# First chunk's down-projection by seven half-size products, its weight sums made in the mixer, its last norms after the second up phase

## The chip, the cores and the metric

The kernel runs on one core of one Trainium2 chip. The metric is the device time of one execution in microseconds (us). Engine names are those of the profile: PE is TensorE's matmuls, PEld its weight loads, DVE is VectorE, ACT is ScalarE, POOL is GpSimd, SP is SyncE, which issues most DMAs. Each engine runs its own queue of instructions in a fixed order and waits on semaphores.

## The reference, cut to what matters

One layer of a streaming encoder over 2048 positions with 1024 features, all in float32: a mixer (a linear recurrence and a gated spatial mixer), then a feed-forward part with a width-3 causal convolution. Each sub-layer is wrapped in two norms and a modulation computed from a vector `c`.

```python
h = rmsnorm(x, g_mix_pre[l]) * (1.0 + sc_m) + sh_m
z = h @ w_in[l]
...
y = y @ w_out[l]
x = x + gt_m * rmsnorm(y, g_mix_post[l])

h = rmsnorm(x, g_ffn_pre[l]) * (1.0 + sc_f) + sh_f
up = causal_depthwise_conv(h @ w_up[l], ffn_conv_w[l], ffn_conv_b[l])
g_ff, v_ff = jnp.split(up, 2, axis=-1)
y = (jax.nn.gelu(g_ff) * v_ff) @ w_down[l]
x = x + gt_f * rmsnorm(y, g_ffn_post[l])
```

The change touches the last three lines: the down-projection (3072 to 1024 features), the norm `g_ffn_post` behind it and the modulation `gt_f`.

## The kernel before, in words

Features lie on partitions, positions on the free axis. Every float32 matmul operand is split into a high and a low half (ACT casts the high half, DVE subtracts to get the low half, line 143), and a product is three matmuls: high by high, high by low, low by high.

The program has these stages. The mixer works in four chunks of 512 positions (about 0 to 680 us). The feed-forward part works in two chunks of 1024 positions, `C` = 0 and 1, each with an up phase (24 steps `f`; a step makes 128 gate and 128 value features, convolves them, applies gelu and multiplies) and a down-projection.

- The up phase multiplies 2 x 2 blocks by seven half-size products instead of eight (`up_pair`), except the first two steps of chunk 0 (`up_plain`). A step's result `gg` is stored to `gd` by SP (`gated`).
- Chunk 0's down-projection is plain (`down(0, t)`): for each half `t` of 512 positions, 24 steps of 8 output blocks, 3 matmuls each.
- Chunk 1's down-projection (`down_fast(1)`) uses seven products of half size. The block indices are even and odd feature blocks by output and position halves. Its products are called by their operands: "11" by "11", "s1" by "t1", "s2" by "t2", "s4" by "22", "s3" by "t3", "12" by "21", "22" by "t4". Each has 6 steps `q` of 24 matmuls (144 in all). They accumulate in two sets of four PSUM banks, `A` and `B`.
- The `s` operands are sums of gate products. `g_sums` makes them for chunk 1 on DVE in its up phase and stores them to `gsd`. The `t` operands are sums of weights. `w_sums` makes them on POOL and stores them to `wsd`: eight of the twelve pairs from the raw weights that the plain stage loads anyway (`W_SUMS`), four in the second up phase (`w_sums_apart`).
- `final` is the last norm: a reciprocal (line 206), eight scalings of 128x512 (line 1164), four adds of the residual (line 1169) and four stores. Chunk 0's first norm runs in the second plain half; its second one runs in the second up phase, from step 3 on, with its data read back from `od`.
- `ada_task(5, 1)` computes the modulation `gt_f`: eight passes of 128x1024 on DVE (line 280) with waits between them.

Work in the background is written as generators in a list; `tick()` advances each by one step, and `drain()` runs what is left to its end at that place. A scheduler then orders each engine's queue; `tc.high_priority(offset=...)` moves operands ahead. Buffers are pools of 4 KB per partition: 36 for general use (`t4`), 8 for split weights (`wp`), 4 for raw weights (`rw`), 3 for loads (`lp`). An instruction that reuses a buffer waits for its last reader.

Of the kernel before, what the change touches and what calls it, by code (L numbers as in the profile page):

```python
# [40 lines left out]
def block_kernel(ctx: ExitStack, tc: tile.TileContext, xt, cols, rows, wada, wada_r, win_k, win_s, win_v, wgate, wsp, wout, wup, wdown, out):  # L41
# [586 lines left out]


# [439 lines left out]
    W_SUMS = (7, 9, 11), (4, 5, 6, 8, 10)  # L1069
    done = []  # L1070
    od = dram.tile([P, ND, 512], F32, name="od")

    def down(C, t):


        n = f"{C}{t}"
        sl = slice(512 * t, 512 * t + 512)
        pts = {}
        G, W = {}, {}
        by_dram = t == 1  # L1080
        last_f = 2
        raws = {}

        def operands(f):
            if f % 2 == 0:
                with tc.high_priority(offset=150):
                    raw = rw.tile([P, 2, 512], F32, tag="wraw", name=f"gr{n}_{f}")
                    sync.dma_start(out=raw, in_=gd[C, :, f:f + 2, sl])
                    hl = [wp.tile([P, 2, 512], F32R, tag="w", name=f"g{q}{n}_{f}") for q in "hl"]
                    split(hl[0], hl[1], raw, "act")  # L1090
                for b in range(2):
                    G[f + b] = hl[0][:, b], hl[1][:, b]

            def mkraw(name):
                raws[f] = rw.tile([P, 8, P], F32, tag="wraw", name=name)
                return raws[f]

            W[f] = weight(wdown[f], [P, 8, P], f"wd{n}_{f}", ahead=150, mkraw=mkraw)
            if f % 2 and f // 2 in W_SUMS[t]:
                with tc.high_priority(offset=150):  # L1100
                    w_sums(f // 2, raws[f - 1], raws[f])

        def mm(f, d):
            if d not in pts:
                pts[d] = bank(f"dn{n}_{d}")
            wh, wl = W[f]
            mm3(pts[d], (wh[:, d], wl[:, d]), G[f], f == 0, f == NF - 1)

        O, acc = [], []

        def evict(d):
            if d % 2 == 0:
                O.append(t4(f"fo{n}_{d}"))
            acc.append(e_tile(f"fs{n}_{d}"))
            act.activation(out=acc[-1], in_=pts[d], func=AF.Square)
            o = O[-1][:, d % 2]
            act.copy(out=o, in_=pts[d])
            if d:
                vec.tensor_tensor(out=acc[0], in0=acc[0], in1=acc[-1], op=ALU.add)
            if by_dram and d % 2:  # L1120
                sync.dma_start(out=od[:, d - 1:d + 1], in_=O[-1])

        for f in range(2):
            operands(f)
            for d in range(7):
                mm(f, d)
            tick()
        while done:
            drain(done.pop(0))
# [289 lines left out]
```

## Time and profile before

| what | value |
|---|---|
| median of 3 runs | 2149.26 us (2148.96 to 2150.14) |
| profiled execution, its own time | 2147.84 us |
| its span | 2146.1 us |
| mixer, to the first up step | about 680 us |
| first up phase | about 680 to 1150 us |
| plain down-projection, both halves | 1150 to 1424 us |
| second up phase | 1424 to 1882 us |
| seven-product down-projection | 1890 to 2121 us |
| end of the last norm | 2146 us |

The span is the profiler's time from the first to the last instruction of that one execution; the median is of separate runs. Busy time of PE counts overlapping matmuls by their modelled ends, so PE's pace is read from the starts of neighbouring matmuls.

### The profile page before, as it was taken

The page shows a single profiled execution, that of the slowest core. Times are in us where ns is not written, and L with a number is a line of the kernel's source. Part 1 is how long each engine was busy: PE and PEld are TensorE (multiplying, and loading weights), DVE is VectorE, ACT ScalarE, POOL GpSimd, SP SyncE. Part 2 cuts the span into 40 slices and gives each one's busy share as a digit, 9 for nine tenths or more (in the row PEclk, how much of TensorE's full clock was granted, in tenths as well). Part 3 has the DMA queues.
Part 4 walks back from the last instruction along what each step waited for, and adds up shares of the span by engine and source line. Part 5 has one row for each costly group of instructions (what it writes and reads, how often), then busy time and mean ns, then how long its engine had stood idle before and what let it go on. Part 6 is the DMA issues. An engine that isn't in the chain of part 4 may idle for free.

```text
span 2146.1 us, 24188 instructions
## 1 busy us (share of the span) xinstructions
PE 2029.0 (95%) x8888; PEld 1667.2 (78%) x8888; DVE 1486.8 (69%) x1631; ACT 943.4 (44%) x1214; POOL 526.3 (25%) x322
## 2 busy tenths in 40 slices
PE   5897979999998999999999999999999999989995
PEld 3686868878877888787788887788888888868884
DVE  7787698697575688988987637745665555564556
ACT  3463643633644455554555434443333333353442
POOL 4355244343212234435330031430011110000000
PEclk8899989999999999999999999999999999999997
DMA  8587578677586679889875756657898887576645
GB/s 326 177 308 279 185 261 288 247 252 280 199 295 224 214 264 325 303 293 349 295 294 190 247 196 220 231 182 241 301 335 297 301 282 242 201 253 208 197 157 147
DMA packets 176359, 541.01 MB, mean 252 GB/s; under 512 B 16496, under 2 KB 16624, under 8 KB 176240
## 3 DMA queue, kind: packets, MB, share of 16 engines
q1 hardware_dynamic: 164176, 496.47, 66.5%
q0 software_dynamic: 10912, 38.80, 4.8%
q10 hardware_dynamic: 1152, 4.19, 0.5%
q8 instruction: 70, 1.15, 0.2%
q14 instruction: 49, 0.40, 0.1%
HBM read 355.90 MB, written 184.55 MB: 252 GB/s over the span
## 4 chain that ended last, share of the span: by engine, by line
PE 75%; DVE 11%; DMA 5%; issue 4%; ACT 4%; POOL 1%; SPq 0%; DVEq 0%; ACTq 0%; POOLq 0%
PE upa L980 7%; PE upa L982 7%; PE upa L981 7%; PE dA L1233 5%; PE dB L1233 5%; PE dn L179 4%; PE dn L181 4%; PE dn L180 4%; PE upc L980 3%; PE upc L981 3%; PE upc L982 3%; PE upb L981 2%; PE upb L982 2%; PE upb L980 2%; PE lg L179 1%
## 5 line engine op out<-in xcount | busy, mean ns | idle before, releaser
L929 DVE SCALAR_TENSOR_TENSOR a<-Rg,prm,a 128x1023 f32<-128x1023 f32 x92 | 128.9, 1401 | 97.8 <-ACT a L927 97.8
L929 DVE SCALAR_TENSOR_TENSOR a<-Rv,prm,a 128x1023 f32<-128x1023 f32 x92 | 133.0, 1445 | 23.3 <-ACT a L927 22.5
L179 PE MATMUL dn<-gh,wd_h 128*128 128x512 f32 x384 | 147.7, 390 | 1.2 <-ACT fr_r L205 0.8
L180 PE MATMUL dn<-gl,wd_h 128*128 128x512 f32 x384 | 147.3, 389 | 0.0
L181 PE MATMUL dn<-gh,wd_l 128*128 128x512 f32 x384 | 131.5, 390 | 2.3 <-DVE wd_l L143 2.3
L927 ACT ACTIVATE a<-Rv,prm 128x1024 f32<-128x1024 f32 x46 | 57.2, 1244 | 132.4 <-DVE Rv L1048 132.2
L143 DVE TENSOR_TENSOR wd_l<-wd_r,wd_h 128x1024 fp32r<-128x1024 f32 x48 | 59.6, 1244 | 75.8 <-ACT wd_h L138 69.2
L138 ACT CAST wd_h<-wd_r 128x1024 fp32r<-128x1024 f32 x48 | 50.5, 1056 | 129.8 <-PE dn L180 119.1
L1166 POOL DMA_DIRECT2D out_dram<-do x2 | 2.5, 1240 | 409.8 <-DVE do L1164 409.7
L960 POOL TENSOR_TENSOR wug<-wuv,wug 128x512 f32<-128x512 f32 x24 | 41.9, 1747 | 243.6 <-DVE w L143 243.6
L143 DVE TENSOR_TENSOR wt<-wug,wt 128x512 fp32r<-128x512 f32 x72 | 72.5, 1007 | 32.7 <-ACT wt L138 32.6
L985 ACT ACTIVATE a<-a 128x1024 f32<-128x1024 f32 x48 | 50.9, 1061 | 87.4 <-DVE a L929 46.9
L138 ACT CAST wt<-wug 128x512 fp32r<-128x512 f32 x72 | 44.9, 623 | 96.1 <-POOL wug L960 38.8
L181 PEld LDWEIGHTS dn<-gh,wd_l 128*128 128x128 f32 x384 | 71.8, 188 | 18.6 <-DVE wd_l L143 3.8
L179 PEld LDWEIGHTS dn<-gh,wd_h 128*128 128x128 f32 x384 | 72.1, 188 | 17.5 <-ACT wd_h L138 1.3
L180 PEld LDWEIGHTS dn<-gl,wd_h 128*128 128x128 f32 x384 | 72.1, 188 | 14.8
L1175 POOL TENSOR_TENSOR wsr<-wsr 128x512 f32<-128x512 f32 x4 | 5.2, 1296 | 251.5 <-DMA wsr<-in_wdown_dram 251.5
L222 POOL TENSOR_TENSOR rp_s<-rp_s,rp_s 128x1024 f32<-128x1024 f32 x12 | 31.4, 2618 | 116.2 <-ACT rp_s L218 116.0
L1175 POOL TENSOR_TENSOR wd_r<-wd_r 128x512 f32<-128x512 f32 x8 | 11.2, 1396 | 195.8 <-DVE wd_l L143 195.8
L927 ACT ACTIVATE a<-Rg,prm 128x1024 f32<-128x1024 f32 x46 | 57.1, 1242 | 1.3
L1048 DVE TENSOR_TENSOR Rv<-upa,m 128x512 f32<-128x512 f32 x46 | 31.5, 684 | 36.3 <-PE upa L982 36.3
L280 DVE SCALAR_TENSOR_TENSOR ada_m<-wada,cact,ada_m 128x1024 f32<-128x1024 f32 x28 | 47.8, 1706 | 11.9 <-DMA wada<-in_wada_r_dram 11.9
(648 smaller groups left out, 6695.8 us busy)
## 6 DMA issues: line engine op xcount, KB each, us to landing
wkd<-wt SPq DMA_DIRECT2D x88, 512.0 KB, 3.6
wkd<-w SPq DMA_DIRECT2D x66, 512.0 KB, 4.1
w<-wkd SPq DMA_DIRECT2D x66, 512.0 KB, 4.4
wd_r<-in_wdown_dram SPq DMA_DIRECT2D x48, 512.0 KB, 4.4
wrt<-wkd SPq DMA_DIRECT2D x44, 512.0 KB, 4.3
wt<-wkd SPq DMA_DIRECT2D x44, 512.0 KB, 4.6
wada<-in_wada_r_dram SPq DMA_DIRECT2D x32, 512.0 KB, 4.9
win_h<-kept_s SPq DMA_DIRECT2D x30, 512.0 KB, 6.0
```

The costliest lines, as they stand in the source:

```text
L138: act.copy(out=hi, in_=src)
L143: (leng or vec).tensor_tensor(out=lo, in0=src, in1=hi.bitcast(F32), op=ALU.subtract)
L179: pe.matmul(out=out, lhsT=wh, rhs=mh, start=first, stop=False)
L180: pe.matmul(out=out, lhsT=wh, rhs=ml, start=False, stop=False)
L181: pe.matmul(out=out, lhsT=wl, rhs=mh, start=False, stop=last)
L927: act.activation(out=a, in_=R, func=AF.Identity, scale=w[2], bias=col("ffn_conv_b", blk))
L929: vec.scalar_tensor_tensor(out=a[:, s:], in0=R[:, :FT - s], scalar=w[t], in1=a[:, s:], op0=ALU.mult, op1=ALU.add)
L980: pe.matmul(out=pt, lhsT=wh, rhs=mh, start=first and not more and k == 0, stop=False, skip_group_check=more)
L981: pe.matmul(out=pt, lhsT=wh, rhs=ml, start=False, stop=False, skip_group_check=more)
L982: pe.matmul(out=pt, lhsT=wl, rhs=mh, start=False, stop=last and k == 3, skip_group_check=more)
L985: act.activation(out=g, in_=g, func=AF.Gelu_apprx_tanh)
L1233: pe.matmul(out=pt, lhsT=x[:, a, d], rhs=y[:, a], start=first and z == 0, stop=stop and z == 2, skip_group_check=True)
```

## The change

1. `down`, `W_SUMS` and `w_sums_apart` go. Chunk 0 also uses `down_fast`.
2. `w_sums` becomes a background task of the mixer, started at its chunk 2, with its own loads of the weights into the raw-weight buffers `rw`.
3. `g_sums` also runs in chunk 0's up phase, and `gg` of chunk 0 moves into the load buffers `lp`.
4. In `down_fast(0)` the activations' raw tiles are in `t4` and their halves in the weight buffers `wp`. Results go to `od`, the sums of squares into one tile `fsum`. `h2_next` makes the second chunk's input sums in that stage.
5. `first_finals` (the modulation, then both last norms of chunk 0, their data read back from `od`) starts at step 3 of the second up phase. What of it is not reached by then comes out in a `drain()` ahead of `down_fast(1)`.
6. In the last product of chunk 1 the work of `then` starts one step earlier, and its tiles are taken when they are needed.

```diff
@@ mixer
+    def w_sums():
+        for p in range(NF // 2):
+            e, o = [rw.tile([P, 8, P], F32, tag="wraw", name=f"ws{p}_{i}") for i in range(2)]
+            sync.dma_start(out=e, in_=wdown[2 * p])
+            sync.dma_start(out=o, in_=wdown[2 * p + 1])
+            yield
+            pool.tensor_tensor(out=e[:, :4], in0=e[:, 4:], in1=e[:, :4], op=ALU.subtract)
...
+            pool.dma_start(out=wsd[p, 0], in_=e)
+            pool.dma_start(out=wsd[p, 1], in_=o)
+            yield
...
         if c == 2:
             m4, = start(ada_task(4, 1))
+            wst = start(w_sums())
@@ gated
-        o = lp.tile([P, 2, 512], F32, tag="ld", name=f"gg{C}_{f}") if C else g.rearrange("p (a c) -> p a c", a=2)
+        o = lp.tile([P, 2, 512], F32, tag="ld", name=f"gg{C}_{f}")
...
-        if C:
-            GG[f] = o
-            if f % 2:
-                start(g_sums(f // 2))
+        GG[f] = o
+        if f % 2:
+            start(g_sums(C, f // 2))
@@ down_fast, operands
-                raw = t4(f"dgr{n}") if first else lp.tile([P, 2, 512], F32, tag="ld", name=f"dgr{n}")
+                raw = t4(f"dgr{n}") if first or C == 0 else lp.tile([P, 2, 512], F32, tag="ld", name=f"dgr{n}")
                 sync.dma_start(out=raw, in_=a_src(op, q))
-                g = h4(f"dgh{n}"), h4(f"dgl{n}")
+                if C == 0:
+                    g = [wp.tile([P, 2, 512], F32R, tag="w", name=f"dg{x}{n}") for x in "hl"]
+                else:
+                    g = h4(f"dgh{n}"), h4(f"dgl{n}")
@@ down_fast, product
-                if q == 2 and then:
+                if q == (1 if held else 2) and then:
                     then()
@@ down_fast, end for chunk 0
+        if C == 0:
+            run("22", "t4", A, False, 0, lambda: combine(B, "m1", 0, 0))
+            combine(A, None, 1, 0)
+            return
@@ new
+    def first_finals():
+        yield from ada_task(5, 1)
+        vec.tensor_tensor(out=gf, in0=modc[:, 40:48], in1=colr("g_ffn_post", 0, 8), op=ALU.mult)
+        for t in range(2):
+            hl = rms_split(fsum[0][:, t], f"fr0{t}")
+            yield
+            yield from final(0, t, [None] * 4, hl)
...
+    def h2_next():
+        for i in range(2):
+            yield from wait(4)
+            g = h2_sums(1, i, from_x2(1, i), True)
+            for _ in g:
+                yield from wait(2)
@@ main
-    for t in range(2):
-        start(h2_sums(1, t, from_x2(1, t), True), *(() if t else (ada_task(5, 1),)))
-        down(0, t)
-        drain()
...
-    up_phase(1, 0, lambda f: start(done.pop(0)) if f == 3 else start(w_sums_apart()) if f == 8 else None)
+    start(h2_next())
+    down_fast(0)
+    drain()
+    up_phase(1, 0, lambda f: start(first_finals()) if f == 3 else None)
+    drain()
     down_fast(1)
     drain()
```

Three places show how the queues move. The first is DVE where the second up phase ends and the second chunk's first product begins. `a..` are convolution results, `dgl` and `dw.._l` the low halves of activations and weights (in the changed kernel with the chunk's number in front, so `dgl11_0` becomes `dgl111_0`), `gg` the step's product, `fr00` and `fr01` the first chunk's norm factors, `fo` its data and `fx` its residual. DVE before:

```order
L929 SCALAR_TENSOR_TENSOR a1_23_13622<-Rg1_23_13561,prm_81,a1_23_13622 128x1022
L934 SCALAR_TENSOR_TENSOR a1_23_13622<-ftails_4095,prm_81,a1_23_13622 128x2
L143 TENSOR_TENSOR dgl11_0_13657<-dgr11_0_13654,dgh11_0_13656 128x1024
L988 TENSOR_TENSOR gg1_23_13629<-a1_23_13622,a1_47_13603 128x1024
L143 TENSOR_TENSOR dw11_0_l_13663<-dw11_0_r_13660,dw11_0_h_13662 128x1024
L143 TENSOR_TENSOR dgl11_1_13699<-dgr11_1_13696,dgh11_1_13698 128x1024
L143 TENSOR_TENSOR dgl11_2_13735<-dgr11_2_13732,dgh11_2_13734 128x1024
```

DVE now, from the first reciprocal on:

```order
L206 RECIPROCAL fr00_r_13633<-fr00_r_13633 128x512
...
L1104 SCALAR_TENSOR_TENSOR fo00_0_13636<-fo00_0_13636,gf_109,fr00_r_13633 128x512 x2
...
L1104 SCALAR_TENSOR_TENSOR fo00_3_13660<-fo00_3_13660,gf_109,fr00_r_13633 128x512 x2
L1005 TENSOR_TENSOR gg1_23_13610<-a1_23_13603,a1_47_13584 128x1024
L206 RECIPROCAL fr01_r_13674<-fr01_r_13674 128x512
L143 TENSOR_TENSOR dgl111_0_13726<-dgr111_0_13723,dgh111_0_13725 128x1024
L1109 TENSOR_TENSOR fo00_0_13636<-fo00_0_13636,fx00_0_13638 128x1024
...
L1104 SCALAR_TENSOR_TENSOR fo01_0_13677<-fo01_0_13677,gf_109,fr01_r_13674 128x512 x2
...
L1104 SCALAR_TENSOR_TENSOR fo01_3_13701<-fo01_3_13701,gf_109,fr01_r_13674 128x512 x2
L143 TENSOR_TENSOR dw111_0_l_13732<-dw111_0_r_13729,dw111_0_h_13731 128x1024
...
L1109 TENSOR_TENSOR fo01_3_13701<-fo01_3_13701,fx01_3_13703 128x1024
L143 TENSOR_TENSOR dgl111_2_13798<-dgr111_2_13795,dgh111_2_13797 128x1024
```

Both norms now stand between the convolution and the low halves of the first product, and the low half of step 2's activations stands behind the last residual add.

The second place is SP's queue at the same seam; `dgr` and `dw.._r` are the raw loads, `out` the results. SP before:

```order
L1223 DMA dgr11_0_13654<-gd_99 128x2x512
L148 DMA dw11_0_r_13660<-in_wdown_dram 128x2x512
L1223 DMA dgr11_1_13696<-gd_99 128x2x512
L1223 DMA dgr11_2_13732<-gd_99 128x2x512
L989 DMA gd_99<-gg1_23_13629 128x1024
L148 DMA dw11_1_r_13702<-in_wdown_dram 128x2x512
```

SP now:

```order
L1142 DMA dgr111_0_13723<-gd_99 128x2x512
L1101 DMA fx00_0_13638<-x2d_98 128x2x512
L1006 DMA gd_99<-gg1_23_13610 128x1024
L148 DMA dw111_0_r_13729<-in_wdown_dram 128x2x512
L1142 DMA dgr111_1_13759<-gd_99 128x2x512
L1110 DMA out_0_dram<-fo00_0_13636 128x2x512
...
L1101 DMA fx01_2_13695<-x2d_98 128x2x512
L1110 DMA out_0_dram<-fo01_0_13677 128x2x512
L1101 DMA fx01_3_13703<-x2d_98 128x2x512
L1142 DMA dgr111_2_13795<-gd_99 128x2x512
```

The first weight's load moves behind the store of the last step's product, and the load of step 2's activations behind the residual loads and the stores of results.

The third place is POOL in the mixer, around the chain of chunk 2 that ends in its two norms (`r` times the gate, `rl_s` and `rg_s` the sums of squares). POOL before:

```order
L387 TENSOR_TENSOR xc_1_2398<-xc_1_2398,i_1_2809 128x1024
L510 TENSOR_TENSOR r_0_2787<-r_0_2787,gg_0_2726 128x1024
L510 TENSOR_TENSOR r_1_2808<-r_1_2808,gg_1_2785 128x1024
L222 TENSOR_TENSOR rl_s_3086<-rl_s_3086,rl_s_3088 128x1024
L222 TENSOR_TENSOR rg_s_3129<-rg_s_3129,rg_s_3131 128x1024
```

POOL now:

```order
L637 TENSOR_TENSOR ws_0_3906<-ws_0_3906 128x512
L510 TENSOR_TENSOR r_0_2787<-r_0_2787,gg_0_2726 128x1024
L638 TENSOR_TENSOR ws_0_3906<-ws_1_3907,ws_0_3906 128x512
L639 TENSOR_TENSOR ws_1_3907<-ws_1_3907,ws_0_3906 128x512
L641 DMA wsd<-ws_0_3906 128x1024
L640 TENSOR_TENSOR ws_1_3907<-ws_1_3907 128x512
L642 DMA wsd<-ws_1_3907 128x1024
L510 TENSOR_TENSOR r_1_2808<-r_1_2808,gg_1_2785 128x1024
L222 TENSOR_TENSOR rl_s_3090<-rl_s_3090,rl_s_3092 128x1024
L637 TENSOR_TENSOR ws_0_4060<-ws_0_4060 128x512
L222 TENSOR_TENSOR rg_s_3139<-rg_s_3139,rg_s_3141 128x1024
```

The subtractions of the weight pairs and their stores now stand between the instructions of that chain; such pairs run from the mixer's first output projection to its second.

## Rows read from the trace of the kernel before

**Rows 1.** The page's busy table: us, share of the span, instructions.
```profile
PE 2029.0 (95%) x8888; PEld 1667.2 (78%) x8888; DVE 1486.8 (69%) x1631; ACT 943.4 (44%) x1214; POOL 526.3 (25%) x322
```

**Rows 2.** PE's waits: us in total, times, longest; 1424 to 1895, then the mixer.
```profile
PE dA L1233 <- ACT dw_h L138: 6.8, 1, 6.8
PE upa L980 <- DVE Rv L1048: 0.8, 1, 0.8
...
PE rl_m L202 <- DVE rl_hl L142: 13.8, 2, 10.5
```

**Rows 3.** PE's waits from 1150 to 1430 us, the plain down-projection.
```profile
PE dn L181 <- DVE wd_l L143: 2.3, 3, 1.0
PE dn L179 <- ACT fr_r L205: 0.8, 1, 0.8
PE dn L179 <- ACT wd_h L138: 0.5, 2, 0.2
```

**Rows 4.** Timeline of PE: start, duration; the first and the seventh of seven matmuls.
```profile
1424.05 0.39 PE L980 MATMUL upa<-h_10h,w 128*128 128x512 f32 x1
...
1425.41 0.39 PE L980 MATMUL upa<-h_11h,w 128*128 128x512 f32 x1
```

**Rows 5.** The page's groups: count, busy us, mean ns, idle before.
```profile
L179 PE MATMUL dn<-gh,wd_h 128*128 128x512 f32 x384 | 147.7, 390 | 1.2 <-ACT fr_r L205 0.8
...
L1175 POOL TENSOR_TENSOR wd_r<-wd_r 128x512 f32<-128x512 f32 x8 | 11.2, 1396 | 195.8 <-DVE wd_l L143 195.8
```

**Rows 6.** Timeline from the last up matmul to the second product of the second down-projection.
```profile
1882.39 0.39 PE L982 MATMUL upa<-h_11h,wt 128*128 128x512 f32 x1
...
1884.70 1.28 DVE L929 SCALAR_TENSOR_TENSOR a<-Rg,prm,a 128x1023 f32<-128x1023 f32 x1 [0.97 <-ACT a L927]
...
1887.36 1.22 DVE L143 TENSOR_TENSOR dgl<-dgr,dgh 128x1024 fp32r<-128x1024 f32 x1
...
1889.58 0.79 PE L1233 MATMUL dA<-dgh,dw_h 128*128 128x512 f32 x1 [6.80 <-ACT dw_h L138]
...
1891.03 0.63 PE L1233 MATMUL dA<-dgl,dw_h 128*128 128x512 f32 x1
...
1891.45 0.63 PE L1233 MATMUL dA<-dgh,dw_h 128*128 128x512 f32 x1
...
1893.17 0.69 DVE L1000 TENSOR_TENSOR gg<-gg,gg 128x512 f32<-128x512 f32 x1
...
1894.80 0.39 PE L1233 MATMUL dA<-dgh,dw_h 128*128 128x512 f32 x1
...
1924.74 0.39 PE L1233 MATMUL dB<-dghs,dws_h 128*128 128x512 f32 x1
```

**Rows 7.** Timeline of DVE: parts of a last norm of the first chunk.
```profile
1498.88 3.35 DVE L206 RECIPROCAL fr_r<-fr_r 128x512 f32<-128x512 f32 x1 [0.50 <-ACT fr_r L205]
...
1523.22 1.41 DVE L1164 SCALAR_TENSOR_TENSOR fo<-fo,gf,fr_r 128x512 f32<-128x512 f32 x2
1524.67 1.23 DVE L1169 TENSOR_TENSOR fo<-fo,fx 128x1024 f32<-128x1024 f32 x1
```

**Rows 8.** Busy time by engine in 250 to 500 us, clock, DMA share, GB/s.
```profile
250.00:500.00 250.00, 235.61 (x1058) 194.34 (x1058) 214.55 (x219) 116.91 (x136) 91.75 (x47) 0.97 0.71 255
```

**Rows 9.** The same for two periods of the first up phase.
```profile
959.00:978.00 19.00, 18.85 (x84) 15.28 (x83) 16.75 (x17) 9.80 (x16) 9.39 (x5) 1.00 0.99 350
...
1054.00:1073.00 19.00, 19.00 (x86) 15.67 (x85) 18.75 (x19) 11.92 (x18) 5.73 (x4) 1.00 0.77 266
```

**Rows 10.** The page's DMA issues: count, KB each, us to landing.
```profile
wd_r<-in_wdown_dram SPq DMA_DIRECT2D x48, 512.0 KB, 4.4
```

**Rows 11.** The modulation's passes (ns min/median/max) in two stretches; POOL at the first.
```profile
L280 DVE SCALAR_TENSOR_TENSOR ada_m<-wada,cact,ada_m x2: 3415/3416/3417, 384.9 to 442.5; 128x1024 f32<-128x1024 f32 x2
...
384.63 2.58 POOL L613 TENSOR_TENSOR oo<-oo,xr 128x1024 f32<-128x1024 f32 x1
...
L280 DVE SCALAR_TENSOR_TENSOR ada_m<-wada,cact,ada_m x7: 1279/1284/1286, 1188.1 to 1211.5; 128x1024 f32<-128x1024 f32 x7
```

More of the change, by code (lines that the diff above doesn't have):

```diff
@@ L1067, in up_phase @@
         drain(before)
[L1069 to L1129, printed above, removed]
-        for f in range(2):
-            mm(f, 7)
-        for f in range(2, NF - last_f):
-            operands(f)
-            for d in range(8):
-                mm(f, d)
-            tick()
-        for f in range(NF - last_f, NF):
-            operands(f)
-        for d in range(8):
-            for f in range(NF - last_f, NF):
-                mm(f, d)
-            evict(d)
-            tick()
-        hl = rms_split(acc[0], f"fr{n}")
-        done.append(final(C, t, O, hl, by_dram=by_dram))
@@ L1271, in down_fast @@
-        O = [[t4(f"do{t}_{j}") for j in range(4)] for t in range(2)]
-        def combine(pts, other, t, j0):
-            for d in range(4):
-                o = O[t][j0 + d // 2][:, d % 2]
-                vec.tensor_tensor(out=o, in0=pts[d], in1=other[d // 2][:, d % 2], op=ALU.add)
-                square(t, o, f"{t}{j0}{d}")
-        A = [bank(f"dA{d}") for d in range(4)]
-        B = [bank(f"dB{d}") for d in range(4)]
-        m1, m5, x0 = [[t4(f"dk{i}_{j}") for j in range(2)] for i in range(3)]
@@ new lines, in square, with combine @@
+            e = e_tile(f"ds{C}{name}")
+            act.activation(out=e, in_=src, func=AF.Square)
+            vec.tensor_tensor(out=acc[t], in0=acc[t], in1=e, op=ALU.add)
+        def combine(pts, other, t, j0, ds=range(4)):
+            for d in ds:
+                j = j0 + d // 2
+                if d % 2 == 0:
+                    O[t][j] = t4(f"do{C}{t}_{j}")
+                o = O[t][j][:, d % 2]
+                if other:
+                    vec.tensor_tensor(out=o, in0=pts[d], in1=kept[other][d // 2][:, d % 2], op=ALU.add)
+                    square(t, o, f"{t}{j0}{d}")
+                else:
+                    square(t, pts[d], f"{t}{j0}{d}")
+                    if d % 2 and C:
+                        vec.tensor_copy(out=o, in_=pts[d])
+                    else:
+                        act.copy(out=o, in_=pts[d])
+                if C == 0 and d % 2:
+                    sync.dma_start(out=od[t, :, 2 * j:2 * j + 2], in_=O[t][j])
@@ new lines, in down_fast @@
+        A = [bank(f"dA{C}{d}") for d in range(4)]
+        B = [bank(f"dB{C}{d}") for d in range(4)]
+        run("11", "11", A, True)
+        run("s1", "t1", B, True, 0, lambda: keep(A, "m1"))
+        run("s2", "t2", A, False, 0, lambda: keep(B, "m5"))
+        run("s4", "22", B, False, 0, lambda: keep(A, "x0"))
+        run("s3", "t3", A, False, 0, lambda: combine(B, "x0", 0, 2))
+        run("12", "21", B, True, 0, lambda: combine(A, "m5", 1, 2))
+        if C == 0:
+            run("22", "t4", A, False, 0, lambda: combine(B, "m1", 0, 0))
+            combine(A, None, 1, 0)
+            return
@@ L1289, in first_half, with final0 @@
+        def final0():
+            yield
+            yield from final(C, 0, O[0], rms_split(acc[0], "fr10"), pt=B[0])
         def first_half():
[L1290 to L1291 removed]
+            combine(B, "m1", 0, 0)
+            start(final0())
         for d in product("22", "t4", A, False, 2, first_half):
[L1294 to L1299 removed]
+            combine(A, None, 1, 0, (d,))
```

74 lines of the change are left out of this document (25 added, 49 removed).

## The prediction

> **What bounds the kernel now.** I read the busy table of the page first. TensorE (PE) is busy 2029 us of a span of 2146.1, VectorE (DVE) 1487 [rows 1]. The reader is to see that PE is the bound nearly everywhere, so that a matmul taken out is worth its full time, and that any stall put into PE costs its full length.
>
> Then PE's waits, by stage. In the second up phase and the entry of the second down-projection there are two entries: 0.8 us and one wait of 6.8 us for a weight's high half [rows 2]. In the plain down-projection of the first chunk three entries make 3.6 us [rows 3]. So the stages that the change touches run PE almost without a hole, except at one seam: the place where an up phase ends and a down-projection of seven products begins.
>
> Then that seam in the timeline [rows 6]. The last up matmul starts at 1882.39. DVE still has the last convolution (1884.70 on), the multiply and the first low half (1887.36) to do, ACT casts the weight only after the last gelu, and the first product matmul starts at 1889.58. The first 12 matmuls come 0.43 us apart, until 1894.80, behind an idle PE. The second product (dB) starts at 1924.74. Without a loss it would start 145 matmuls after 1882.39. One matmul is (1425.41 - 1424.05) / 6 = 0.2267 us [rows 4], so that would be 1915.26: **the seam costs 9.5 us**.
>
> **The change, part by part.** The sum is made on the profiled execution (2147.84 us; the median of the runs is 2149.26, 1.42 more).
>
> *Matmuls.* The plain stage has three groups of 384 [rows 5]: 1152. Seven products of 144 are 1008. 144 x 0.2267 = **-32.6 us**. The PE order confirms it: 144 rows fewer in all.
>
> *The entry and inside of the first chunk's new down stage.* Before, the end of the first up phase and the plain stage are laid into each other, with no wait at the join [rows 3]. Now it enters as the second chunk does: +9.5 by the seam above. Inside, the operands' halves sit in eight buffers, four to a step of 24 matmuls (5.44 us), so two steps are in hand; DVE needs 2 x 1.22 us a step for low halves (at 1887.36) [rows 6], besides the second chunk's input sums. I put 1.5 us of waits there, and the 3.6 of before go. **+7.4**, from +2 (half the seam) to +13 (each of some five stretches with sums loses a us).
>
> *The seam after the second up phase, where both last norms of the first chunk now stand.* This is the term that decides. The wait counts in the modulation task (21 steps, begun at the fourth of 24) put its end behind the last step of the up phase, so both norms are emitted when the phase is drained. The order shows it: ahead of the low half of the first weight DVE now has two reciprocals, 16 scalings and an add. Before, the same norms stood in the first and the second plain stage and the middle of the up phase, where PE did not feel them.
>
> What DVE has to do, by rows: the reciprocal 3.35, a pair of scalings 1.41, an add of 1024 columns 1.23 [rows 7]; the two splits of the sums about 1.1 each, estimated from a 512-column pass of 0.69 and a shorter cast [rows 6]. Both norms: 6.7 + 8 x 1.41 + 8 x 1.23 + 2.2 = 30.0 us.
> I replay the in-order queues from t = 0 at the last up matmul:
> - convolution of the value half, of the gate half and the splits, reciprocal of the first norm to 8.7; eight scalings to 15.1; the multiply to 16.3.
> - SyncE (SP): the load of the first weight stands behind the store of that product. Issue near 17, landing 4.4 us later [rows 10], cast: first product matmul at 22.5 (before: 7.2).
> - DVE goes on: second reciprocal 19.7, low half 20.9, add and sum 22.8, eight scalings 28.4, then the low half of the first weight, 29.6. PE, after 8 matmuls, stands until then. Step 0 ends at 35, step 1 near 40.
> - Step 2's activations use the three load buffers that the eight residual tiles also pass through. SP has their load behind six residual loads and five stores of results, each store behind its add on DVE. One round (issue, landing 4.4, add 1.23) is near 6 us; the load goes out near 49, lands at 53.5, its low half is ready at 56. Four steps of 5.44 follow: product 1 ends near 79, where before it ended at 1924.74 - 1882.39 - 0.2 = 42.1.
> **+37 us.** Lower end: if no load were ever late, DVE's own work alone would still be 5.3 (convolution) + 30.0 + 1.23 + 4 x 0.69 + 12 x 1.22 = 53.9, and the last step of 5.4 behind it: 59.3, **+17**. Upper end: every restart again at half spacing (24 x 0.2 us, three times) gives **+52**. I take 37, since the replay uses only rows and leaves little slack in it.
>
> *Weight sums in the mixer.* Twelve pairs: 48 subtractions on GpSimd (POOL) at 1.40 us [rows 5] = 67 us, 24 stores, 24 loads, 25.2 MB. They fall in about 250 to 500 us. There DVE is busy 214.6 of 250 us, POOL 91.8, and the queues move 255 GB/s [rows 8]; the most that a row shows is 350 [rows 9]. The sums add 101 GB/s: the stretch would stand at the highest rate seen, with no slack. On POOL the order puts two sums between the gate product, its square sums and the norm: PE has waited for that chain before, 13.8 us in two waits [rows 2]. The low end is +2 (one sum of 1.4 us on that chain), the high end +25 (bytes 88.9 MB at 350 GB/s take 254 us, and a late chain once of 10.5 and again). I take **+10**, nearer the low end because PE's matmuls there depend on a few chains only.
>
> DVE also feels POOL. The weighted sum of the modulation takes 1.28 us where POOL is idle and 3.42 where a POOL add of 2.58 us runs beside it [rows 11]. The Trainium skill has a rule on this: in "SBUF — State Buffer", section "Who interferes with whom", a DVE instruction with two SBUF inputs contends with a GpSimd instruction that reads SBUF, and the shared port pair is an exclusive lock. The rows agree here (3.42 is 1.28 plus most of 2.58); what it would make of the sum is the third case below.
>
> *Gate sums of the first chunk in its up phase.* Four DVE additions of 0.69 per pair, 33 us in all, 1.4 us per period of 19.04; stores of 12.6 MB. DVE has 16.8 of 19 in one period and 18.75 in the fullest, and the queues are at 350 GB/s in the former [rows 9]. Most periods hide it, some do not. **+4** (0 to +10).
>
> *Second up phase and tail.* The modulation's eight passes replace sums on POOL and the older norm; the tail is the same instructions. 0 (-2 to +3).
>
> **Sum:** -32.6 + 7.4 + 37 + 10 + 4 = +25.8: 2173.6 for the profiled kind, **2175 us** on the scale of the median.
>
> **Rivals.**
> 1. *Faster.* DVE's work at the late seam overlaps as the lower end has it (+17), the mixer hides its sums (+2), the entry costs half (+4), the gate sums nothing: -9.6, **2140**. For it: the residual loads may run ahead of the adds. Against it: SP's queue is in order, and the stores stand between the loads.
> 2. *No change.* The late seam at 24, the entry 5, the rest 3: 0, **2149**. It needs the loads of step 2 to go out near 36 instead of 49.
> 3. *Much slower, by the mixer.* DVE stands still for POOL's 67 us, as in the row of 3.42: 214.6 + 67 = 281 in a stretch of 250, +32 in place of +10: **2197**. Against it: some of DVE's passes there have one SBUF input, and a POOL pass can be the one that waits.
> That the change leaves the matmuls or places the norms elsewhere is excluded by the order.
>
> **Chances.** Forecast 0.45, rival 1 0.27, rival 2 0.09, rival 3 0.19. The forecast's own range is 2160 to 2190. The range for 8 in 10 reaches into rival 1 and to rival 3: **2134 to 2199**. A measurement of this kernel tells about 0.2% (4.3 us) from no change; by the same cases faster 0.27, same 0.09, slower 0.64.
>
> **What the changed profile would show.** Seven products of 144 in the first chunk; the entry there with one wait of about 7 us. At the late seam: a first product matmul some 22 us after the last up matmul, a wait for the weight's low half, a wait of 10 us or more for the activations of step 2, the second product 79 us after the last up matmul. In 250 to 500 us: PE's hole grows by about 10, POOL near 160 us busy, the rate above 320 GB/s. The prediction fails if the second product starts within 62 us of the last up matmul, or if the mixer's end moves by under 2 or over 25 us.

## The result, and the profile after

The changed kernel takes 2214.82 us (median of 4 runs, 2214.45 to 2217.84), the kernel before 2149.11 on the same chip: a ratio of 1.0308, 95% interval 1.029 to 1.0326. It is slower by 65.7 us. The forecast was 2175 us, in a range that ended at 2199. The sign was right, the size was not, and the time lies outside the range.

The profiled execution took 2214.45 us, its span is 2212.4. The busy table answers to [rows 1]:

```profile
PE 2013.4 (91%) x8744; PEld 1647.6 (74%) x8744; DVE 1565.4 (71%) x1703; ACT 950.1 (43%) x1224; POOL 525.1 (24%) x322
```

POOL's time is the same as before, since its sums were moved and not added. DVE has 72 instructions more than the 1631 of [rows 1] and is busy 79 us longer. To see where the 66 us of the span arise, four marks are enough. The first is the first matmul of the first up phase; it ends the mixer. These rows (count, ns min/median/max, first and last start in us) are of the kernel before and of the changed one:

```profile
L980 PE MATMUL up<-h_00h,w x32: 389/389/793, 679.6 to 722.8; 128*128 128x512 f32 x32
```

```profile
L997 PE MATMUL up<-h_00h,w x32: 389/389/797, 726.1 to 769.1; 128*128 128x512 f32 x32
```

The others are in the timeline of PE (start, duration): the second up phase's first and last matmul, and the first matmuls of the first and second product of the second down-projection. They answer to [rows 4, 6].

```profile
1452.45 0.39 PE L997 MATMUL upa<-h_10h,w 128*128 128x512 f32 x1
...
1910.28 0.39 PE L999 MATMUL upa<-h_11h,wt 128*128 128x512 f32 x1
...
1932.34 0.80 PE L1155 MATMUL dA<-dgh,dw_h 128*128 128x512 f32 x1 [11.96 <-ACT dw_h L138]
...
1991.92 0.39 PE L1155 MATMUL dB<-dgh1s,dw1s_h 128*128 128x512 f32 x1
```

| stretch | before, us | after, us | difference | predicted |
|---|---|---|---|---|
| start to first up matmul (mixer) | 679.6 | 726.1 | **+46.5** | +10 |
| to the first matmul of the second up phase | 744.45 | 726.35 | -18.1 | -21.2 |
| to its last matmul | 458.34 | 457.83 | -0.5 | 0 |
| to the first matmul of the second product | 42.35 | 81.64 | **+39.3** | +37 |
| to the end of the span | 221.4 | 220.5 | -0.9 | 0 |
| sum | 2146.1 | 2212.4 | +66.3 | +25.8 |

Of the 40.5 us by which the sum is off, 36.5 sit in the first line: the mixer's end moved by 46.5 us, and the prediction had named a move of over 25 as a sign that it fails. PE's waits (us in total, times, longest) name the chains, against 13.8 us in two waits before [rows 2]:

```profile
PE rl_m L202 <- DVE rl_hl L142: 22.6, 4, 15.2
PE rg_m L202 <- DVE rg_hl L142: 19.6, 1, 19.6
PE dA L1155 <- ACT dw_h L138: 19.5, 3, 12.0
PE dA L1155 <- ACT dgh L138: 18.1, 1, 18.1
```

The first two are the mixer's norms, released by DVE. The same stretch as in [rows 8] (busy us of PE, PEld, DVE, ACT and POOL with their instructions, then clock, DMA share, GB/s) now reads:

```profile
250.00:500.00 250.00, 201.19 (x897) 165.11 (x895) 216.66 (x178) 98.43 (x115) 154.70 (x110) 0.90 0.81 295
```

POOL's 154.7 us are near the forecast of 160. PE is idle for 48.8 of 250 us where it was idle for 14.4, against a forecast of some 10 more, and the rate is 295 GB/s where over 320 was forecast. DVE is busy as long as before with 178 instructions in place of 219.

Around the longest wait for the first norm (`rl_m`; `rg_m` is the gate norm), the timeline of the changed kernel reads so. The first row lists two DVE passes (ns min/median/max, first and last start), the rest are POOL's and PE's:

```profile
L256 DVE SCALAR_TENSOR_TENSOR x<-x,sm,n_r x2: 737/5832/10926, 300.1 to 311.0; 128x512 f32<-128x512 f32 x2
...
301.59 1.27 POOL L638 TENSOR_TENSOR ws<-ws,ws 128x512 f32<-128x512 f32 x1
302.82 2.33 POOL L143 TENSOR_TENSOR wout_l<-wout_r,wout_h 128x1024 fp32r<-128x1024 f32 x1
305.10 0.57 POOL L171 DMA_DIRECT2D kept_o<-wout_h  x1
305.70 1.27 POOL L637 TENSOR_TENSOR ws<-ws 128x512 f32<-128x512 f32 x1
306.92 2.34 POOL L222 TENSOR_TENSOR rg_s<-rg_s,rg_s 128x1024 f32<-128x1024 f32 x1
309.22 1.26 POOL L639 TENSOR_TENSOR ws<-ws,ws 128x512 f32<-128x512 f32 x1
...
316.30 0.77 PE L202 MATMUL rl_m<-rl_hl,onesD 128*128 128x512 f32 x1 [15.20 <-DVE rl_hl L142]
```

The reader is to see two equal DVE passes, of which one takes 0.74 us and the other, which began at 300.11, 10.93. It came through at 311.03, 0.55 us behind the last of five POOL passes that had begun after it. DVE counts as busy the whole time, so its busy share before [rows 8] was no measure of free time.

The first norm's matmul came only 2 us later for it than before (316.30 against 314.27), since the kernel before has a hold at the same place. The larger loss is at the gate norm just behind. In the kernel before:

```profile
303.83 5.83 DVE L256 SCALAR_TENSOR_TENSOR x<-x,sm,n_r 128x512 f32<-128x512 f32 x2 [3.84 <-DMA x<-in_xt_dram]
...
314.27 0.77 PE L202 MATMUL rl_m<-rl_hl,onesD 128*128 128x512 f32 x1 [10.52 <-DVE rl_hl L142]
...
316.50 0.68 DVE L226 TENSOR_TENSOR rg_s<-rg_s 128x512 f32<-128x512 f32 x1
...
317.79 1.43 PE L202 MATMUL rg_m<-rg_hl,onesD 128*128 128x512 f32 x2 [1.55 <-DVE rg_hl L142]
```

In the changed kernel:

```profile
321.09 3.35 DVE L206 RECIPROCAL rl_r<-rl_r 128x512 f32<-128x512 f32 x1 [1.60 <-ACT rl_r L205]
324.36 1.18 DVE L280 SCALAR_TENSOR_TENSOR ada_m<-wada,cact,ada_m 128x1024 f32<-128x1024 f32 x1
325.46 1.76 DVE L226 TENSOR_TENSOR rg_s<-rg_s 128x512 f32<-128x512 f32 x1
327.14 11.14 DVE L537 SCALAR_TENSOR_TENSOR r<-r,prm,rl_r 128x512 f32<-128x512 f32 x4
...
339.96 0.77 PE L202 MATMUL rg_m<-rg_hl,onesD 128*128 128x512 f32 x1 [19.63 <-DVE rg_hl L142]
```

Two things add up here. Four scalings of `r` take 11.14 us. And DVE's order is another: the gate norm's sum and cast (`rg_s`, `rg_hl`) stood right behind the first norm; now its sum stands behind a reciprocal and a modulation pass, and its cast behind four scalings and a modulation pass more, although POOL's part of it had ended at 309.26. The two norms of this chunk, the second of four, made PE wait 12.5 us before and 37.3 now: 24.8 of the 46.5 us.

### The profile page after: what moved, and what is told of

It is laid out like the page before. It is cut to its first block, busy times and chain, and to the rows that moved or that the text cites. A ratio compares the mean times of both kernels' runs of the same rounds, so it can differ in the third digit from the quotient of the medians.

```text
span 2212.4 us, 24016 instructions
## 1 busy us (share of the span) xinstructions
PE 2013.4 (91%) x8744; PEld 1647.6 (74%) x8744; DVE 1565.4 (71%) x1703; ACT 950.1 (43%) x1224; POOL 525.1 (24%) x322
## 3 DMA queue, kind: packets, MB, share of 16 engines
q10 hardware_dynamic: 1152, 4.19, 0.5%
## 4 chain that ended last, share of the span: by engine, by line
PE 59%; DVE 20%; DMA 7%; issue 6%; ACT 5%; POOL 2%; SPq 0%; DVEq 0%; ACTq 0%; POOLq 0%
PE dA L1155 10%; PE dB L1155 9%; PE upa L997 6%; PE upa L998 5%; PE upa L999 5%; PE upc L997 3%; PE upc L998 3%; PE upc L999 3%; DVE a L946 2%; PE upb L999 1%; PE upb L998 1%; DVE acc L665 1%; PE upb L997 1%; DVE x L256 1%; DMA xr<-in_xt_dram 1%
## 5 line engine op out<-in xcount | busy, mean ns | idle before, releaser
L1155 PE MATMUL dA<-dgh,dw_h 128*128 128x512 f32 x192 | 72.1, 411 | 37.6 <-ACT dw_h L138 19.5
L1155 PEld LDWEIGHTS dA<-dgh,dw_h 128*128 128x128 f32 x192 | 38.0, 199 | 47.4 <-ACT dw_h L138 20.9
L143 DVE TENSOR_TENSOR dgl<-dgr,dgh 128x1024 fp32r<-128x1024 f32 x36 | 43.9, 1221 | 41.2 <-ACT dgh L138 41.2
L1155 PE MATMUL dA<-dgh,dw_l 128*128 128x512 f32 x192 | 70.7, 402 | 2.4 <-DVE dw_l L143 2.4
L1155 PE MATMUL dA<-dgl,dw_h 128*128 128x512 f32 x192 | 72.3, 405 | 0.0
L280 DVE SCALAR_TENSOR_TENSOR ada_m<-wada,cact,ada_m 128x1024 f32<-128x1024 f32 x28 | 50.1, 1789 | 27.6 <-DMA wada<-in_wada_r_dram 27.6
L138 ACT CAST dgh<-dgr 128x1024 fp32r<-128x1024 f32 x36 | 37.8, 1049 | 70.0 <-DMA dgr<-gd 30.0
L143 DVE TENSOR_TENSOR dw_l<-dw_r,dw_h 128x1024 fp32r<-128x1024 f32 x36 | 43.8, 1220 | 25.4 <-ACT dw_h L138 25.3
L1005 DVE TENSOR_TENSOR gg<-a,a 128x1024 f32<-128x1024 f32 x48 | 58.3, 1215 | 2.7 <-ACT a L1002 2.6
L138 ACT CAST dw_h<-dw_r 128x1024 fp32r<-128x1024 f32 x36 | 37.5, 1047 | 45.1 <-DMA dw_r<-in_wdown_dram 16.2
L143 DVE TENSOR_TENSOR dw1s_l<-dw1s_r,dw1s_h 128x1024 fp32r<-128x1024 f32 x24 | 29.3, 1222 | 38.3 <-ACT dw1s_h L138 34.1
```

The lines of the kernel that those rows point to most:

```text
L138: act.copy(out=hi, in_=src)
L143: (leng or vec).tensor_tensor(out=lo, in0=src, in1=hi.bitcast(F32), op=ALU.subtract)
L280: vec.scalar_tensor_tensor(out=flat, in0=w, scalar=cact[:, kt:kt + 1], in1=flat, op0=ALU.mult, op1=ALU.add)
L1155: pe.matmul(out=pt, lhsT=x[:, a, d], rhs=y[:, a], start=first and z == 0, stop=stop and z == 2, skip_group_check=True)
```

## The experiments

Theories for the mixer's 46.5 us, as they were before the runs. *Turns*: DVE's passes wait for POOL's passes, so the subtractions themselves are the price. *Bytes and queues*: the 25 MB, and loads and stores in SP's and POOL's queues, are the price. For the late seam: *the norms' place* against *DVE's work is only moved*. A third cause, the new order of DVE's queue, was not among them; the traces below speak of it. The rows of e1 to e4 and e10 are of one execution each; two executions of one kernel (e9, e12) have their first up matmul at 701.7 and 705.1 us, so differences of some 3 us say little.

**e1: the sums on DVE**, all four subtractions of a pair.

```diff
-            pool.tensor_tensor(out=e[:, :4], in0=e[:, 4:], in1=e[:, :4], op=ALU.subtract)
+            vec.tensor_tensor(out=e[:, :4], in0=e[:, 4:], in1=e[:, :4], op=ALU.subtract)
...
```

> The changed kernel, with the 48 subtractions of the weight sums on DVE in place of POOL; loads and stores stay. The changed kernel's first up matmul is at 726.1 us, that of the kernel before at 679.6. Theory (turns): while POOL's instructions follow one another, a DVE pass with two SBUF inputs gets no turn, and this is the mixer's 46.5 us; then 48 x 0.69 = 33 us more on DVE are far cheaper: first up matmul at 690 to 702, time 2178 to 2192. Rival (bytes and queues): the 25 MB and the loads and stores in SP's and POOL's queues cost it: first up matmul at 715 to 730, time 2203 to 2220.

Measured: 2200.76 us, first up matmul at 709.1. Neither: 17 us better than on POOL, but 29.5 above the kernel before, close to the full 33 us of the added passes. DVE had little time there that PE did not wait for.

**e2: the sums left out, loads and stores kept**: the four subtractions of a pair are removed, so the stored sums are not made.

```diff
-            pool.tensor_tensor(out=e[:, :4], in0=e[:, 4:], in1=e[:, :4], op=ALU.subtract)
...
```

> The changed kernel without the 48 subtractions: the weights are loaded and stored as they are (the sums are left out). Theory (turns): first up matmul at 680 to 690, time 2168 to 2180. Rival (bytes and queues): at 715 to 728, time 2203 to 2217.

Measured: 2171.34 us, first up matmul at 682.3. The transfers alone cost 2.7 us, no more than the spread, though in this run (busy us by engine, clock, DMA share, GB/s) the queues moved more than I held for the most they can:

```profile
350.00:400.00 50.00, 48.03 (x212) 39.43 (x212) 35.47 (x41) 14.64 (x16) 25.98 (x15) 1.00 1.03 411
```

The bytes alone fall as a cause, and with them the bound of 350 GB/s that I took from [rows 9].

**e3: the subtractions alone.** One pair of tiles, E and O_, is loaded once, ahead of the loop, and all pairs subtract within it; no store.

```diff
-            sync.dma_start(out=e, in_=wdown[2 * p])
-            sync.dma_start(out=o, in_=wdown[2 * p + 1])
-            pool.tensor_tensor(out=e[:, :4], in0=e[:, 4:], in1=e[:, :4], op=ALU.subtract)
+            pool.tensor_tensor(out=e[:, :4], in0=E[:, 4:], in1=E[:, :4], op=ALU.subtract)
...
-            pool.dma_start(out=wsd[p, 0], in_=e)
-            pool.dma_start(out=wsd[p, 1], in_=o)
```

> The changed kernel with the 48 subtractions on POOL, but on one pair of weights loaded once, without the 22 other loads and without the 24 stores; the products read raw weights in place of sums. Theory (turns): most of the 46.5 us stays, first up matmul at 705 to 726, time 2194 to 2214. Rival (bytes and queues): at 680 to 690, time 2168 to 2180.

Measured: 2205.21 us, first up matmul at 715.2: 35.6 us of the 46.5 without the sums' transfers. The place is not the same, though: without loads to wait for, POOL makes these sums at 438 to 539 us, in the changed kernel at 294 to 517, and PE's long waits are now at the next chunk's norms. One stretch of this run shows DVE and POOL side by side. First the busy times (PE, PEld, DVE, ACT, POOL), then the rows:

```profile
450.00:500.00 50.00, 18.41 (x77) 14.19 (x75) 49.97 (x26) 15.53 (x18) 50.00 (x27) 0.71 0.50 180
```

```profile
475.95 1.48 DVE L142 CAST rl_hl<-rl_s 128x512 fp32r<-128x512 f32 x1
477.47 2.71 DVE L143 TENSOR_TENSOR rl_hl<-rl_s,rl_hl 128x512 fp32r<-128x512 f32 x1
...
482.31 3.34 DVE L206 RECIPROCAL rl_r<-rl_r 128x512 f32<-128x512 f32 x1
```

```profile
475.44 1.71 POOL L640 TENSOR_TENSOR ws<-wsx,wsx 128x512 f32<-128x512 f32 x1
477.11 2.52 POOL L222 TENSOR_TENSOR rg_s<-rg_s,rg_s 128x1024 f32<-128x1024 f32 x1
...
481.27 2.24 POOL L641 TENSOR_TENSOR ws<-wsx,ws 128x512 f32<-128x512 f32 x1
483.48 1.26 POOL L639 TENSOR_TENSOR ws<-wsx 128x512 f32<-128x512 f32 x1
```

Both engines are "busy" for all of the 50 us, with 26 and 27 instructions, and PE works 18. The two engines take turns: the cast and the subtraction each end 0.3 to 0.6 us after a POOL pass has ended, and the next POOL pass, begun meanwhile, is long in its turn. A subtraction of 0.69 takes 2.71, a cast of 0.42 (its length in e10, below) takes 1.48. The reciprocal, with one input, keeps its 3.34 (3.35 in [rows 7]). POOL pays as well: 1.71 and 2.24 where it has 1.26 beside the reciprocal. PE's wait for the gate norm behind this is 19.2 us, and here too a reciprocal, modulation passes and four scalings stand ahead of that norm's cast on DVE.

**e4: the last norms inside the second up phase.**

```diff
-    def ada_task(m, pause=0):
+    def ada_task(m, pause=0, tail=5):
...
-        yield from wait(5)
+        yield from wait(tail)
...
-        yield from ada_task(5, 1)
+        yield from ada_task(5, 0, 2)
...
-    up_phase(1, 0, lambda f: start(first_finals()) if f == 3 else None)
+    up_phase(1, 0, lambda f: start(first_finals()) if f == 0 else None)
```

> The changed kernel with the first chunk's modulation and last norms begun at step 0 of the second up phase, one step per pass and a shorter pause behind, so that both norms come out inside the phase. Theory: the seam (81.7 us from the last up matmul to the second product, 42.3 before) falls back to 41 to 45 us, the up phase grows by under 3 us, time 2174 to 2181. Rival (DVE's work is only moved): the up phase takes in 20 us or more, time 2195 to 2215.

Measured: 2179.52 us, 35.3 less than the changed kernel. PE's timeline at the seam:

```profile
1913.82 0.39 PE L999 MATMUL upa<-h_11h,wt 128*128 128x512 f32 x1
1921.02 0.80 PE L1155 MATMUL dA<-dgh,dw_h 128*128 128x512 f32 x1 [6.80 <-ACT dw_h L138]
...
1955.48 0.39 PE L1155 MATMUL dB<-dgh1s,dw1s_h 128*128 128x512 f32 x1
```

The seam is 41.7 us again (before 42.35), and the up phase, 1454.09 to 1913.82, is 1.9 us longer. The 39 us of the late seam were the place of the norms and of the modulation ahead of them.

**e5 and e6: the sums later, on POOL and on DVE**, with e4's edit. A gate holds the sums back behind the last sum of squares recorded on the same engine. The diff is e5's; e6 names DVE's last such sum, and `vec` for `pool` in the subtractions.

```diff
-            wst = start(w_sums())
...
+            with tc.issue_after(last["pool"].ins):
+                pool.tensor_tensor(out=e[:, :4], in0=e[:, 4:], in1=e[:, :4], op=ALU.subtract)
...
+    start(w_sums())
     nt = start(mixer_norm(NC - 1, 2))
```

> The changed kernel with both terms taken on: last norms inside the second up phase (as in e4), and the weight sums on POOL again, but queued behind POOL's last square sum of the fourth chunk, so that they run in about 500 to 720 us, where DVE is busy 28 to 36 of 50 us in the kernel before instead of 37 to 46. Theory (turns): the 48 passes still take turns with DVE, some 36 us of it, but DVE has about 85 us free there: first up matmul at 682 to 697, time 2136 to 2151. Rival (the arithmetic costs PE the same wherever it runs in the mixer): first up matmul at 712 to 726, time 2165 to 2180.

> As e5, with the late weight sums on DVE (48 x 0.69 = 33 us) instead of POOL. Theory (turns): DVE's own 33 us fit into its free 85 us there: first up matmul at 682 to 692, time 2136 to 2147, no slower than e5. Rival (DVE is short in the whole mixer): first up matmul at 700 to 712 as in e1, time 2153 to 2165.

Measured: e5 2189.13 us, ratio 1.019 (1.0172 to 1.0208), first up matmul at 738.4; e6 2154.52 us, ratio 1.003 (1.0017 to 1.0042), at 703.0. The theory missed in both. e6 lies in its rival's range (700 to 712, 2153 to 2165), e5 beyond its rival's too. In e5, PE's longest wait and SP's row for the first up weight are:

```profile
PE up L998 <- ACT w L138: 54.2, 1, 54.2
```

```profile
728.78 0.33 SPq L957 DMA_DIRECT2D wug<-in_wup_dram  x1
```

The up phase's raw weights use the four `rw` buffers that the sums' tiles now hold, so their load went out at 728.78. The late place took away one conflict and made another. In e6 SP stands for 6.5 us in front of a load of the sums, with other loads behind it:

```profile
673.87 0.33 SPq L922 DMA_DIRECT2D hs<-hs  x1
680.33 0.33 SPq L635 DMA_DIRECT2D ws<-in_wdown_dram  x1
```

The load of the first up weight behind them goes out at 684.91. (The 689.68 in the expectation of e7 is a row of e5; e6 has none there.)

**e7, e8, e9, e11: other places and buffers** (each with e4's edit, sums on DVE).

```diff
e7 = e6 with
-            sync.dma_start(out=e, in_=wdown[2 * p])
+            pool.dma_start(out=e, in_=wdown[2 * p])
e8 = e4 with the sums on DVE, started ahead of mixer_z(3)
e9 = e6 with
-            e, o = [rw.tile([P, 8, P], F32, tag="wraw", name=f"ws{p}_{i}") for i in range(2)]
+            e, o = [tp.tile([P, 8, P], F32, tag="t4", name=f"ws{p}_{i}") for i in range(2)]
e11 = e9, started ahead of mixer_z(3), behind the last norm sum on DVE
```

> e6 (norms inside the up phase, late sums on DVE; 2154.5 us, first up matmul at 703.0 and a wait of 28 us before it) with the 24 loads of the sums issued by POOL instead of SP. In e6 SP stands from 673.87 to 689.68 in front of such a load, whose buffer is not free, and the loads behind it are late. Theory (SP's queue is the rest of e6's loss): the wait of 28 us falls under 14, first up matmul at 683 to 692, time 2134 to 2144. Rival (the raw buffers themselves are short, whoever issues): first up matmul at 698 to 712, time 2149 to 2165.

> Norms inside the up phase, sums on DVE, begun one chunk later than in the change (ahead of the fourth chunk's input projection), with no order forced, so that they spread over about 340 to 640 us. Theory (DVE's free time decides): half of the 33 us falls where DVE is full, half where it is free: first up matmul at 688 to 700, time 2140 to 2153. Rival (as dear as in e1, 29.5 us): first up matmul at 705 to 712, time 2157 to 2166.

> e6 with the sums' tiles in the 36 general buffers in place of the 4 raw ones. Theory (raw buffers and the queue in front of them): the loads no longer wait, first up matmul at 682 to 692, time 2133 to 2144. Rival (general buffers are just as short there): 698 to 715, time 2149 to 2168.

> e9 (norms inside the up phase, sums on DVE in general buffers; first up matmul at 701.7, a wait of 27.6 us ahead of it while the queues move 414 GB/s in 600 to 650 us) with the sums begun one chunk earlier in the text, behind the third chunk's norm on DVE, so that they run from about 480 us. Theory (late transfers of the next stage, behind the sums' loads and stores, hold the first up matmul): the wait falls under 14 us, first up matmul at 688 to 697, time 2138 to 2148, ratio to the kernel before 0.995 to 1.000. Rival (33 us of DVE cost the same wherever they stand): 700 to 710, time 2150 to 2162.

| run | time, us | first up matmul | PE's wait for the first up matmul |
|---|---|---|---|
| e7 | 2167.08 (one run) | 713.0 | 29.3 |
| e8 | 2159.84 (one run) | 706.5 | 8.6 |
| e9 | 2152.86 (one run) | 701.7 | 27.6 |
| e11 | 2166.95, ratio 1.0086 (1.0062 to 1.011) | 715.7 | 25.8 |

All four theories missed; e8 and e9 lie in their rivals' ranges, e7 and e11 beyond theirs. Neither who issues the loads (e7), nor the raw buffers (e9), nor an earlier start (e11) shortens the wait of some 28 us that comes with late sums by more than 2.2. In e9 it is a late chain of the norm ahead of the up phase: its last load, of `xf`, goes out at 686.78 us (661.84 in the kernel before), and from there to the first up matmul it takes 14.9 us (17.8 before). Why that load is late stays open. e8 has no such wait, but it moved nothing: its sums ran at 297 to 526 us, in e1 at 299 to 528, so it is e1 again with e4's edit. e6 and e9, where DVE was expected to have room, still cost 23.4 and 22.1 us in the mixer.

**e10: POOL passes that only write.** The four subtractions, two loads and two stores of a pair go; four fills of a whole tile stand in their place.

```diff
-            pool.tensor_tensor(out=e[:, :4], in0=e[:, 4:], in1=e[:, :4], op=ALU.subtract)
...
+            for i in range(2):
+                pool.memset(e, 0.5)
+                pool.memset(o, 0.5)
```

> e3 with 48 fills of 128x1024 on POOL in place of its 48 subtractions: POOL's queue keeps 48 extra instructions at the same places, but they write and read nothing (no loads, stores or sums; the products read raw weights). Theory (turns: two-input passes and casts of DVE wait for POOL passes that read): DVE's passes keep their lengths, first up matmul at 680 to 695, time 2170 to 2184. Rival (the longer queue on POOL delays its own square sums, and PE with them): first up matmul at 705 to 720 as in e3 (715.2), time 2194 to 2210.

Measured: 2192.30 us, first up matmul at 698.5. That is between the two: 18.9 us above the kernel before, 16.7 below e3. The fills ran at 292 to 377 us, not where e3's subtractions ran. DVE and POOL of this run, first beside a POOL add, then beside fills:

```profile
306.25 3.86 DVE L260 SCALAR_TENSOR_TENSOR x2lo<-x,modc,x2hi 128x512 fp32r<-128x512 f32 x1
...
318.69 0.75 DVE L260 SCALAR_TENSOR_TENSOR x2lo<-x,modc,x2hi 128x512 fp32r<-128x512 f32 x1
...
353.79 6.56 DVE L142 CAST rp_hl<-rp_s 128x512 fp32r<-128x512 f32 x1
```

```profile
307.20 2.35 POOL L222 TENSOR_TENSOR rg_s<-rg_s,rg_s 128x1024 f32<-128x1024 f32 x1
...
317.18 1.86 POOL L636 MEMSET ws<- 128x1024 f32 x2
...
352.84 1.85 POOL L636 MEMSET ws<- 128x1024 f32 x2
...
358.21 1.85 POOL L637 MEMSET ws<- 128x1024 f32 x2
```

One and the same pass takes 3.86 us where POOL's add runs (it began with a fill ahead of the add) and 0.75 at 318.69, where only fills run. All 13 two-input passes of 512 columns or more that have only fills beside them keep their lengths, 0.68 to 0.75 us for 512. A cast does not: the one at 353.79 ended at 360.35, 0.3 us behind the last of the fills. So POOL's reading is what holds a two-input pass, and fills can hold a cast. The busy time up to the first up matmul agrees, since all these kernels have the same 591 DVE instructions there (e1 has 48 more). The sum rows of the kernel before, of e10, e3 and the changed kernel, in this order:

```profile
sum 679.60, PE 603.78 PEld 494.25 DVE 514.54 ACT 323.86 POOL 244.24; mean PE 301.89 PEld 247.13 DVE 257.27 ACT 161.93 POOL 122.12
```

```profile
sum 698.50, PE 603.76 PEld 493.95 DVE 523.56 ACT 323.55 POOL 285.69; mean PE 301.88 PEld 246.98 DVE 261.78 ACT 161.77 POOL 142.85
```

```profile
sum 715.20, PE 609.85 PEld 498.36 DVE 553.01 ACT 323.31 POOL 322.18; mean PE 304.93 PEld 249.18 DVE 276.51 ACT 161.66 POOL 161.09
```

```profile
sum 726.10, PE 611.30 PEld 497.23 DVE 551.51 ACT 323.91 POOL 328.17; mean PE 305.65 PEld 248.62 DVE 275.76 ACT 161.95 POOL 164.09
```

Forty-eight reading passes on POOL lengthen the same DVE instructions by 37.0 us (551.51 - 514.54), by 38.5 without the transfers; fills by 9.0, of which the one cast is 6.1. In e1, where DVE made the sums itself, its busy time is 552.3. Moving the sums from DVE to POOL thus saves DVE nothing at all there. e10's 18.9 us are for the most part DVE's order. PE's waits for the two norms of the second chunk make 17.6 of them (30.1 us against 12.5), and at the gate norm DVE's queue has the changed kernel's order:

```profile
316.22 1.29 DVE L280 SCALAR_TENSOR_TENSOR ada_m<-wada,cact,ada_m 128x1024 f32<-128x1024 f32 x1 [4.04 <-DMA wada<-in_wada_r_dram]
...
329.28 2.73 DVE L537 SCALAR_TENSOR_TENSOR r<-r,prm,rl_r 128x512 f32<-128x512 f32 x4
...
332.80 0.77 PE L202 MATMUL rg_m<-rg_hl,onesD 128*128 128x512 f32 x1 [11.45 <-DVE rg_hl L142]
```

A modulation pass that waits 4.04 us for its load stands ahead of the first norm's sum, and the four scalings, here unstretched, ahead of the gate norm's cast. So at the gate norm the wait is 1.55 us in the old order, 11.45 in the new one, and 19.63 in the new one with the scalings held (the changed kernel). By these rows, of the 18.1 us lost there about 10 are the order and about 8 the held passes; that is an estimate, since no run has the subtractions on POOL at this norm with the old order. e1 and e2, with no subtractions on POOL, wait 1.6 and 4.6 us at this norm.

**e12: the best of these, timed.**

> e9 again (both terms taken on: norms inside the second up phase, weight sums on DVE in general buffers behind the fourth chunk), timed against the kernel before, since one run of each (2152.9 and 2154.4) does not tell them apart. By the terms: -32.6 + 11.1 - 3.6 (entry and inside) + 7.0 (first up phase) + 2.4 (norms inside the up phase) + 22.1 (first up matmul at 701.7 against 679.6) = +6: ratio 1.001 to 1.005. Rival (the second entry gains as well, since nothing of the first chunk's last norm is near it): 0.996 to 1.000.

Measured: 2152.42 us against 2146.98, ratio 1.0024 (1.0014 to 1.0035), as the terms had it. It is e9's kernel, 62 us better than the change and still 5 slower than the kernel before. No version here beats that one.

## Why the prediction was wrong

- **Matmuls, entry, inside and gate sums: right, 3 us short.** The stretch has -18.1 against -21.2. The first up phase ends at 1212.56, so it lasts 486.5 us; before it was 744.45 - 1152 x 0.2267 - 3.6 = 479.7. The gate sums cost +7 in place of +4. The down stage then lasts 1452.45 - 1212.56 = 239.9 us, 11.4 over 1008 matmuls; I had 9.5 + 1.5. PE's waits in it answer to [rows 3]: one of 6.7 us at the entry and 1.2 us in all the others.
- **The late seam: right.** The first product matmul came 22.06 us after the last up matmul (22.5 in the replay), the second product 81.64 (79). The wait for step 2's activations, which I put at 10 us or more, is 18.1. The replay of in-order queues with measured lengths was good to 3 us, and e4 shows that the place of the norms and their modulation is what is in it.
- **The mixer: wrong, and this is the step that failed.** The prediction put +10, "nearer the low end because PE's matmuls there depend on a few chains only"; it measured +46.5. Four things in it were false. The free time: I read DVE's 214.6 of 250 us [rows 8] as 35 us to spare, but those busy times hold waiting for POOL, and the norms that PE waits for are made on DVE one behind the other. e1 shows what a microsecond of DVE is worth there: 29.5 for 33, transfers included. The price of a pass: the row of 3.42 us beside POOL's 2.58 [rows 11] said that a DVE pass waits a POOL pass out; I gave that to the third rival instead of the sum. The bytes, on which I spent the upper bound, cost 2.7 (e2). And the order: I read POOL's new queue in the mixer and not DVE's, in which the gate norm now stands behind other work; with fills in place of the subtractions that order still costs most of 18.9 us (e10).
- **The third rival had one of the two mechanisms and still was too cheap.** It let DVE stand for POOL's 67 us and gave +32 by DVE's free time. DVE lost 37.0 us, and PE 46.5; the order of DVE's queue was in no rival. Subtractions alone cost 35.6 (e3), at another place and at other norms, transfers alone 2.7 (e2); together 8 more than the sum of both. POOL waited 27.1 us for the sums' loads in 250 to 520 us of the changed kernel and not at all for such loads before, and its square sums are queued behind; that this makes the 8 us was not tried. The 22 us of the 46.5 that lie outside the second chunk's norms were not taken apart.
- **The range.** It ended at 2199, just above the third rival's 2197, which had the other terms at their middle. A case that kills the free time of an engine must be priced with that engine as the bound, not by what it had left over.

On the rule that was weighed: the Trainium skill ("SBUF — State Buffer", section "Who interferes with whom") says that a two-input DVE pass contends with a GpSimd instruction that reads SBUF and not with one that only writes it, and that casts can contend by another mode, DVE's two-port modes. The runs agree: a subtraction of 0.69 us took 2.71 beside reading passes (e3), and a two-input pass kept its 0.75 beside fills (e10); a cast of 0.42 took 1.48 beside reading passes (e3) and 6.56 beside fills (e10); the one-input reciprocal is unchanged. The same section says, of the two-port modes, that whoever issues first has the port for the whole instruction; in the changed kernel a two-input DVE pass was held through five POOL passes that had begun after it (301.59 to 310.48 us), so the one that waits does not always come next.

## What to carry to other kernels

Subtractions moved from VectorE to GpSimd were not off VectorE here (551.5 us busy against 552.3): where VectorE is on the path, price each such pass at its own length on VectorE, and look for a stage where VectorE is not waited for. A busy share that holds stretched passes (0.86 here) does not tell the free time; compare the length of a pass with its shortest elsewhere in the trace before calling the rest free. When a scheduler writes the queues, read the new order of every engine on the path, and not only of the one that gets the work. A background task that does not end before its stage does comes out in one block at the stage's end: count its steps, and replay the in-order queues from that point.
